# Two adaLN units of the first feed-forward summed on VectorE beside the first output product, with the conditioning row loaded earlier

## Chip, cores and metric

The kernel runs on one core of one Trainium2 chip. The metric is the device time of one execution in microseconds (us); the time before is 2353.25 us, the median of 3 runs (2352.32 to 2356.36).

## What is computed

One inference step of a two-layer backbone, for 128 prompt tokens (context pass) and 128 latent tokens (denoising) at once, D = 2048, all in fp32. Layer 0 mixes by MLA beside grouped-query attention with one input and one output projection, layer 1 by differential attention; each is followed by a gated convolutional feed-forward. Every sub-layer is modulated (adaLN) by shift, scale and gate, which are themselves a product of the conditioning vector:

```python
mod = jax.nn.silu(cond) @ w_ada[l] + b_ada[l]
sh1, sc1, gt1, sh2, sc2, gt2 = jnp.split(mod[:, None, :], 6, axis=-1)
h = rmsnorm(x, g_norm_mix[l]) * (1 + sc1) + sh1
m, new = mixer(h, ...)            # its last step is ... @ w_out_ab[i] in layer 0
x = x + gt1 * m
h = rmsnorm(x, g_norm_ffn[l]) * (1 + sc2) + sh2
x = x + gt2 * conv_ffn(h, w_ffn_up[l], w_ffn_conv[l], b_ffn_conv[l], w_ffn_down[l])
```

`cond` has two values, one for each group of tokens, so `mod` is two rows of 6 x 2048 numbers per layer.

## The kernel before, in words

**Products.** Activations lie feature-major: 16 blocks of 128 features by 256 tokens (128 prompt, 128 latent). Weights come as 1 MB tiles of 16 blocks 128x128 (`raw`, 3 buffers) by DMA from SyncE. Each fp32 value is kept as two float32r parts. For weights, `split` (L219) makes the high part on ScalarE (`wh`, the cast at L221) and the low part on VectorE (`wl`, a subtraction at L222), 8 blocks at a time, into 4 buffers of each; so half a product's weights are one cast and one split. `gemm` (L324) makes one output block of 128 features from 16 weight blocks with three matmuls each (L338 wh by high, L339 wh by low, L342 wl by high), 48 in all, into one of three accumulators `acc`. `residual` (L615) adds accumulator times gate to `x` on VectorE, two instructions at L617, which frees the accumulator; `stat_add` then squares and sums on ScalarE (L172) and GpSimd (L176).

**Modulation.** `mod` is cut into units (l, j, q): layer, which of the six vectors, which 512 of its 2048 numbers; j = 3 and 4 are shift and scale of the feed-forward, 5 its gate. A unit reads 4 tiles of 1 MB (`araw`, two buffers). There are two ways to make one.
- A *row unit* (list ROWS): TensorE multiplies the conditioning columns by each tile (`sum_rows`, L452: 4 matmuls a tile, which the profile shows as 8 records), then ScalarE copies the sum (L394), TensorE turns it by 4 transposes (L401), and VectorE reduces it (L403) and adds the bias (L411).
- A *feature unit* (list FEATS): VectorE multiplies each tile by the broadcast conditioning row and sums it over the free axis, one instruction per tile and row of `cond` (`feature_sum`, L429: 8 per unit, 128x2048 each, and a short read-out). It needs `condb`, the row on all partitions: `load_row` (L420) loads 2 MB (L422) and applies Silu on ScalarE in two instructions (L424). Early in the kernel the same memory serves as a tile buffer for row units (L498), last read by matmuls of L452.

**Pacing.** After each product `pump` (L515) advances row units by a rate of RATE and feature units by a rate of FRATE; RLIMIT and FLIMIT say how many units a stage may finish. `ensure` finishes what a stage needs. The order on each engine is then set by a scheduler, which places instructions by a simulated timeline; only what is marked to be kept in program order stays as written (among it load_row and feature_sum).

**The stages around the change.** In the in-projection (`mixer_ab`, quarter q == 3) the caches are loaded and the last quarter of the normed input is modulated. Then come the heads, then the first output product, out0 for short: 16 products in a loop, of which the last three are quiet (no pump) with the split in halves of a half (FINE). In these products the second half of the 16 blocks is consumed first (`first=8`), since the heads that make it are done first; products 0 to 2 begin beside the last heads. Then `modulated` hands over to the feed-forward: it finishes the statistics, makes one more row unit (0, 5, 0) in the gap (two tiles ahead of the new products), casts the modulated `hx` in 16 pieces, and runs three products at once (`first_three`), L324, L325 and L326. In the feed-forward, `up` calls load_row after its third block.

Of the kernel before, what the change touches and what calls it, by code (L numbers as in the profile page):

```python
# [10 lines left out]
F32 = mybir.dt.float32  # L11
F32R = mybir.dt.float32r
BF16 = mybir.dt.bfloat16
# [5 lines left out]
P = 128  # L19
D = 2048  # L20
KD = D // P
T = 128
NT = 2 * T
# [46 lines left out]
ROWS += [(0, j, q) for j in (2, 4, 3) for q in range(4)]  # L70
# [4 lines left out]
FEATS = [(0, 5, 1), (0, 5, 2), (0, 5, 3)]  # L75
# [3 lines left out]
RLIMIT = {"ab": 20, "ffn0": 21, "c": 32, "ffn1": 33}  # L79
FLIMIT = {"ab": 0, "ffn0": 12, "c": 12, "ffn1": 15}  # L80
SUMMED = [22, 23, 24, 26, 27, 28, 31]
# [4 lines left out]
def step_kernel(ctx: ExitStack, tc: tile.TileContext, A: dict):  # L86
# [346 lines left out]
    def feature_step():  # L433

        l, j, q = FEATS[feat["i"]]
        t, c = divmod(feat["t"], 2)
        if c == 0:
            feat["raw"] = T_(wpool, [P, 4, 512], "araw", bufs=2)
            sp.dma_start(out=feat["raw"], in_=A["w_ada"][l, j, q, t])
        feature_sum((l, j, q), t, c, feat["raw"],  # L440
                    T_(feat["pool"], [P, D], "junk").rearrange("p (g n) -> p g n", g=4))
# [243 lines left out]
    def mixer_ab(hx, rb0, st):  # L685
        l = 0
        with tc.tile_pool(name="ab", bufs=1) as ab:
            with tc.tile_pool(name="abp", bufs=1) as pj:
# [145 lines left out]
                for q in range(1, 4):  # L834
# [84 lines left out]
        ensure(l, 2)  # L919
        ada["pew"] = PEW["out0"]  # L920
        W = Weights(A["w_out_ab"], KD, 1)
        oh, ol = (lambda k: o[:, k, :NT]), (lambda k: o[:, k, NT:2 * NT])
        for c in range(KD):
            fine[0] = c >= KD - QUIET[1]
            residual(gemm(W.chunk(), oh, ol, first=8), l, 0, c, st)
            pump(RATE["out0"] if c < KD - QUIET[1] else 0)
# [124 lines left out]
    def ffn(hx, W, ready, todo, l, st):  # L1051
# [4 lines left out]
        with tc.tile_pool(name=f"ffn{l}", bufs=1) as fp, banks(f"pffn{l}") as pf:  # L1056
# [22 lines left out]
            def up(q):  # L1079
                gs = []  # L1080
                for i in range(q * KQ, (q + 1) * KQ):
# [11 lines left out]
                    if l == 0 and i == LATE - 1:  # L1093
                        load_row()
# [197 lines left out]
```

## Time and profile before

| | us |
|---|---|
| three runs, median (lowest to highest) | 2353.25 (2352.32 to 2356.36) |
| the profiled execution, its own time | 2353.05 |
| its span in the trace | 2351.3 |
| PE / weight loads / DVE / ACT / POOL busy | 2304.8 / 2190.2 / 1780.2 / 1163.3 / 144.8 |
| granted TensorE clock, mean | 0.993 |
| DMA, mean | 260 GB/s |

The span is what lies between the first and the last recorded instruction; the execution took 1.75 us more. PE is TensorE, PEld its weight loads, DVE VectorE, ACT ScalarE, POOL GpSimd, SP SyncE. In a timeline row stand the start, the time from start to end, the engine, line and operation, the tiles (`out<-in`), the shape and a count; behind it, if it waited, the idle time and what ended it. Matmuls overlap: one of 0.28 us starts every 0.11 us. So what an instruction costs TensorE is read from the distance of starts, not from its length.

### The profile page before, as it was taken

The numbers are of one execution on the slowest core, as the hardware profiler recorded it, in microseconds if no ns is written. First come the engines' busy times: TensorE is split into PE (matmuls) and PEld (weight loads), VectorE is DVE, ScalarE is ACT, GpSimd is POOL, SyncE is SP. The second block draws the span as 40 slices with busy tenths as digits, with TensorE's granted clock in tenths as the row PEclk, the third lists the DMA queues.
The fourth block names the chain that finished last, engine by engine and source line by source line (L and its number), as shares of the span: only waits on it lengthen the run. The fifth ranks groups of instructions, "written<-read, shape, count | busy, mean of one in ns | idle before, by whom it ended". The sixth has DMA issues, their size and how long they took to land. (4 is left out here: it accounts for less than half of the span.)

```text
span 2351.3 us, 47128 instructions
## 1 busy us (share of the span) xinstructions
PE 2304.8 (98%) x19654; PEld 2190.2 (93%) x19654; DVE 1780.2 (76%) x2662; ACT 1163.3 (49%) x1835; POOL 144.8 (6%) x133
## 2 busy tenths in 40 slices
PE   7999999999999999999999999999999999999997
PEld 6788878799999999999989999898999999999997
DVE  3667554579999999999968889887899755666654
ACT  4346553465554355554455555446555434555542
POOL 0002001100000000001220000022000000000011
PEclk9999999999999999999999999999999999999998
DMA  9887778777777877777767788786677555555553
GB/s 383 338 324 261 256 277 315 306 290 267 267 269 272 309 263 257 264 262 271 293 235 256 262 310 298 300 316 243 221 265 269 198 194 190 192 196 198 196 188 118
DMA packets 92421, 610.81 MB, mean 260 GB/s; under 512 B 9968, under 2 KB 17840, under 8 KB 20528
## 3 DMA queue, kind: packets, MB, share of 16 engines
q1 hardware_dynamic: 92208, 607.80, 70.2%
q8 instruction: 154, 2.52, 0.4%
q14 instruction: 59, 0.48, 0.1%
HBM read 603.01 MB, written 4.75 MB: 258 GB/s over the span
## 5 line engine op out<-in xcount | busy, mean ns | idle before, releaser
L221 ACT CAST wh<-raw 128x1024 fp32r<-128x1024 f32 (+1 forms) x788 | 793.4, 1013 | 947.5 <-PE acc L339 765.1
L222 DVE TENSOR_TENSOR wl<-raw,wh 128x1024 fp32r<-128x1024 f32 (+1 forms) x788 | 922.6, 1186 | 345.2 <-ACT wh L221 326.2
L338 PE MATMUL acc<-hx,wh 128*128 128x256 f32 x3808 | 1058.9, 279 | 5.6 <-ACT hx L568 4.6
L339 PE MATMUL acc<-hx,wh 128*128 128x256 f32 x3808 | 1056.4, 278 | 0.6 <-DVE hx L553 0.6
L342 PE MATMUL acc<-hx,wl 128*128 128x256 f32 x3808 | 1056.5, 278 | 0.0
L338 PEld LDWEIGHTS acc<-hx,wh 128*128 128x128 f32 x3808 | 715.8, 188 | 32.4 <-issue 10.9
L342 PEld LDWEIGHTS acc<-hx,wl 128*128 128x128 f32 x3808 | 716.1, 188 | 10.3 <-issue 9.2
L339 PEld LDWEIGHTS acc<-hx,wh 128*128 128x128 f32 x3808 | 716.8, 188 | 6.3 <-issue 5.0
L429 DVE CUSTOM_DVE_ANT_0 junk<-araw,condb 128x2048 f32<-128x2048 f32 (+1 forms) x176 | 404.0, 2295 | 0.0
L339 PE MATMUL acc<-g,wh 128*128 128x256 f32 x1408 | 388.3, 276 | 0.0
L342 PE MATMUL acc<-g,wl 128*128 128x256 f32 x1408 | 388.0, 276 | 0.0
L338 PE MATMUL acc<-g,wh 128*128 128x256 f32 x1408 | 387.8, 276 | 0.0
L339 PEld LDWEIGHTS acc<-g,wh 128*128 128x128 f32 x1408 | 264.3, 188 | 0.0
L342 PEld LDWEIGHTS acc<-g,wl 128*128 128x128 f32 x1408 | 264.1, 188 | 0.0
L338 PEld LDWEIGHTS acc<-g,wh 128*128 128x128 f32 x1408 | 264.0, 188 | 0.0
L176 POOL TENSOR_TENSOR sqacc<-sqacc,sq 128x256 f32<-128x256 f32 x62 | 83.4, 1344 | 1579.5 <-issue 1291.6
L1066 ACT ACTIVATE cv<-acc,convw 128x256 f32<-128x256 f32 x176 | 98.4, 559 | 3.6 <-PE acc L342 2.0
L617 DVE SCALAR_TENSOR_TENSOR x<-acc,mod,x 128x128 f32<-128x128 f32 x192 | 58.1, 344 | 54.7 <-PE acc L342 54.1
L1069 DVE SCALAR_TENSOR_TENSOR cv<-acc,convw,cv 128x254 f32<-128x254 f32 x176 | 83.8, 476 | 4.6 <-ACT cv L1066 4.6
L1072 DVE SCALAR_TENSOR_TENSOR cv<-acc,convw,cv 128x254 f32<-128x254 f32 x176 | 84.4, 480 | 3.7
L452 PE MATMUL ada<-araw,condw 128*32 128x512 f32 x576 | 79.3, 616 | 4.5 <-DMA araw<-w_ada 4.5
L303 PE MATMUL acc<-wh,hx 128*128 128x256 f32 x256 | 70.3, 281 | 0.9 <-ACT dv L977 0.9
(238 smaller groups left out, 2125.6 us busy)
## 6 DMA issues: line engine op xcount, KB each, us to landing
araw<-w_ada SPq DMA_DIRECT2D x178, 1024.0 KB, 5.5
raw<-w_up SPq DMA_DIRECT2D x176, 1024.0 KB, 4.8
raw<-w_down SPq DMA_DIRECT2D x88, 1024.0 KB, 4.8
raw<-w_in_c SPq DMA_DIRECT2D x48, 1024.0 KB, 6.0
raw<-w_in_ab SPq DMA_DIRECT2D x19, 1024.0 KB, 7.2
raw<-w_out_ab SPq DMA_DIRECT2D x16, 1024.0 KB, 6.9
raw<-w_out_c SPq DMA_DIRECT2D x16, 1024.0 KB, 6.1
condb<-w_ada SPq DMA_DIRECT2D x12, 1024.0 KB, 7.1
```

The source lines that it names most:

```text
L176: pool.tensor_tensor(out=st["acc"], in0=st["acc"], in1=sq, op=ALU.add)
L221: pin(act.copy(out_hi, src))
L222: pin(dve.tensor_tensor(out=out_lo, in0=src, in1=out_hi.bitcast(F32), op=ALU.subtract))
L303: pe.matmul(ps, hi, wh[:, s], start=a, stop=False)
L338: fixed(pe.matmul(ps[:, :n], wh, xh(k), start=(i == 0), stop=False))
L339: fixed(pe.matmul(ps[:, :n], wh, xl(k), start=False, stop=False))
L342: fixed(pe.matmul(ps[:, :n], wl, xh(k), start=False, stop=(i == last)))
L429: tc.keep_in_program_order(dve.tensor_tensor_reduce(out=junk, in0=raw, in1=condb[:, c].rearrange("p (g n) -> p g n", g=4), scale=1.0, scal ...
L452: i = pe.matmul(ada["ps"][32 * g:32 * g + 32, :], condw[:, 4 * t + g, :], raw[:, g], start=(t == 0), stop=(t == 3), skip_group_check=True)
L1066: pin(act.activation(y, ps, AF.Identity, scale=cw[:, 1, m:m + 1], bias=cw[:, 3, m:m + 1]))
L1069: pin(dve.scalar_tensor_tensor(out=y3[:, :, 1:], in0=p3[:, :, :T - 1], scalar=cw[:, 0, m:m + 1], in1=y3[:, :, 1:], op0=ALU.mult, op1=ALU.add))
L1072: pin(dve.scalar_tensor_tensor(out=y3[:, :, :T - 1], in0=p3[:, :, 1:], scalar=cw[:, 2, m:m + 1], in1=y3[:, :, :T - 1], op0=ALU.mult, op1=A ...
```

## The change

Units (0, 3, 2) and (0, 3, 3), half of the feed-forward's shift in layer 0, leave ROWS and become the first two of FEATS, so that they are summed by VectorE; their tiles in `w_ada` are laid out transposed by the host like those of other feature units. Limits and the indices in SUMMED shift by two. In out0 the row rate falls from 1.2 to 0.7 a product, and a feature rate of 1.3 comes in (16 sums over the 13 products that are not quiet). A pool `abo` around out0 holds two more `araw` buffers and the sums' unused output (`junk`, bf16). `ensure` for shift and scale of the feed-forward moves to the end of that loop. load_row moves from the third block of the feed-forward to the last quarter of the in-projection, right behind the loads of the caches. From there on, lines of the changed kernel are 1 to 3 higher.

```diff
-RATE = {"in": 0.5, "in3": 0.25, "heads": 0.85, "out0": 1.2, "c": 0.7, "outc": 0.7}
-FRATE = {"up": 0.7, "down": 1.42}
+RATE = {"in": 0.5, "in3": 0.25, "heads": 0.85, "out0": 0.7, "c": 0.7, "outc": 0.7}
+FRATE = {"out0": 1.3, "up": 0.7, "down": 1.42}
...
-ROWS += [(0, j, q) for j in (2, 4, 3) for q in range(4)]
+ROWS += [(0, j, q) for j in (2, 4) for q in range(4)] + [(0, 3, 0), (0, 3, 1)]
...
-FEATS = [(0, 5, 1), (0, 5, 2), (0, 5, 3)]
+FEATS = [(0, 3, 2), (0, 3, 3)]
+FEATS += [(0, 5, 1), (0, 5, 2), (0, 5, 3)]
...
-RLIMIT = {"ab": 20, "ffn0": 21, "c": 32, "ffn1": 33}
-FLIMIT = {"ab": 0, "ffn0": 12, "c": 12, "ffn1": 15}
+RLIMIT = {"ab": 18, "ffn0": 19, "c": 30, "ffn1": 31}
+FLIMIT = {"ab": 2, "ffn0": 14, "c": 14, "ffn1": 17}
...
-            feat["raw"] = T_(wpool, [P, 4, 512], "araw", bufs=2)
+            feat["raw"] = T_(feat["pool"] if l == 0 and j == 3 else wpool, [P, 4, 512], "araw", bufs=2)
...
                     if q == 3:
                         caches()
+                        load_row()
...
-        ensure(l, 2)
-        ada["pew"] = PEW["out0"]
-        W = Weights(A["w_out_ab"], KD, 1)
+        with tc.tile_pool(name="abo", bufs=1) as feat["pool"]:
+            ensure(l, 2)
+            ada["pew"] = PEW["out0"]
+            W = Weights(A["w_out_ab"], KD, 1)
...
-            residual(gemm(W.chunk(), oh, ol, first=8), l, 0, c, st)
-            pump(RATE["out0"] if c < KD - QUIET[1] else 0)
+                residual(gemm(W.chunk(), oh, ol, first=8), l, 0, c, st)
+                pump(*((RATE["out0"], FRATE["out0"]) if c < KD - QUIET[1] else (0,)))
+            ensure(l, 4)
+            ensure(l, 3)
...
-                    if l == 0 and i == LATE - 1:
-                        load_row()
```

How the order on the engines moves, at three places. First VectorE at the start of out0, before: residuals of the first products (`acc`) and splits of the next ones (`wl`).

```order
L617 SCALAR_TENSOR_TENSOR x_76<-acc_3848,mod_77,x_76 128x128 x2
L222 TENSOR_TENSOR wl_4064<-raw_4057,wh_4063 128x1024
L617 SCALAR_TENSOR_TENSOR x_76<-acc_3917,mod_77,x_76 128x128 x2
L222 TENSOR_TENSOR wl_4133<-raw_4130,wh_4132 128x1024
L617 SCALAR_TENSOR_TENSOR x_76<-acc_3987,mod_77,x_76 128x128 x2
L222 TENSOR_TENSOR wl_4137<-raw_4130,wh_4136 128x1024
L222 TENSOR_TENSOR wl_4207<-raw_4204,wh_4206 128x1024
L617 SCALAR_TENSOR_TENSOR x_76<-acc_4067,mod_77,x_76 128x128 x2
L222 TENSOR_TENSOR wl_4211<-raw_4204,wh_4210 128x1024
```

The same place after; `junk` is the unused output of a sum, and the second row of each pair is its read-out.

```order
L618 SCALAR_TENSOR_TENSOR x_76<-acc_3854,mod_77,x_76 128x128 x2
L430 ISA junk_3909,mod_77<-araw_3907,condb_82 128x2048
L430 ISA mod_77 128x1
L618 SCALAR_TENSOR_TENSOR x_76<-acc_3921,mod_77,x_76 128x128 x2
L223 TENSOR_TENSOR wl_4064<-raw_4057,wh_4063 128x1024
L618 SCALAR_TENSOR_TENSOR x_76<-acc_3993,mod_77,x_76 128x128 x2
L223 TENSOR_TENSOR wl_4132<-raw_4129,wh_4131 128x1024
L430 ISA junk_3981,mod_77<-araw_3907,condb_82 128x2048
L430 ISA mod_77 128x1
L223 TENSOR_TENSOR wl_4136<-raw_4129,wh_4135 128x1024
L223 TENSOR_TENSOR wl_4212<-raw_4209,wh_4211 128x1024
L430 ISA junk_4055,mod_77<-araw_4053,condb_82 128x2048
```

Sums now stand between the residuals and the splits; the first is directly behind the first residual, and the split `wl_4064`, which stood behind that residual, comes behind the sum and the second residual.

Second, TensorE at the hand-over, before: the tiles of a row unit (`araw`), the statistics (L201, L202), the spread of the scale over partitions (L216), and the feed-forward's first matmuls (L324).

```order
L452 MATMUL ada_5004<-araw_4784,condw_79 32x512 x4
L452 MATMUL ada_5004<-araw_5002,condw_79 32x512 x4
L201 MATMUL att_5039<-cst_74,sqacc_3899 128x1
L202 MATMUL att_5039<-cst_74,sq_5000 128x1
L216 MATMUL att_5056<-diag_5053,cst_74 128x256
L452 MATMUL ada_5004<-araw_5009,condw_79 32x512 x4
L452 MATMUL ada_5004<-araw_5015,condw_79 32x512 x4
L324 MATMUL acc_5168<-hx_5038,wh_5171 128x256
```

After, where L402 is the turn of unit (0, 3, 1) and `misc` the sum of unit (0, 5, 0):

```order
L453 MATMUL ada_4718<-araw_4791,condw_79 32x512 x4
L453 MATMUL ada_4718<-araw_5003,condw_79 32x512 x4
L202 MATMUL att_5028<-cst_74,sqacc_3905 128x1
L203 MATMUL att_5028<-cst_74,sq_5001 128x1
L402 MATMUL ada_5015<-cst_74,am_5013 128x128 x4
L217 MATMUL att_5045<-diag_5042,cst_74 128x256
L453 MATMUL misc_5037<-araw_5023,condw_79 32x512 x4
L325 MATMUL acc_5157<-hx_5027,wh_5160 128x256
L453 MATMUL misc_5037<-araw_5025,condw_79 32x512 x4
```

One tile of L453 is left between the spread and the first matmul L325, the next stands behind three of these, and the transposes of the unit before stand ahead of the spread.

Third, the loads that SyncE issues in the in-projection, before: `raw` are weights, `araw` modulation tiles, `vg` a cache.

```order
L704 DMA vg_236<-cache_gqa_v 128x256
L267 DMA raw_1789<-w_in_ab 128x2048
L267 DMA raw_1884<-w_in_ab 128x2048
L267 DMA raw_1983<-w_in_ab 128x2048
L469 DMA araw_1819<-w_ada 128x2048
L469 DMA araw_1915<-w_ada 128x2048
```

After:

```order
L705 DMA vg_236<-cache_gqa_v 128x256
L268 DMA raw_1792<-w_in_ab 128x2048
L268 DMA raw_1887<-w_in_ab 128x2048
L423 DMA condb_82<-condb 128x4096
L268 DMA raw_1986<-w_in_ab 128x2048
L470 DMA araw_1822<-w_ada 128x2048
L470 DMA araw_1918<-w_ada 128x2048
```

The 2 MB load of `condb` stands ahead of the weight load that was third. On ScalarE its two Silu instructions stand between the cast `wh_1893` of the tile before it and the statistics of the projection:

```order
L222 CAST wh_1889<-raw_1887 128x1024
L569 CAST hx_223<-nt_1780 128x256
L569 CAST hx_223<-nt_1786 128x256
L222 CAST wh_1893<-raw_1887 128x1024
L425 ACTIVATE condb_82<-condb_82 128x2048 x2
L170 ACTIVATE sqacc_1816<-proj_241 128x256
L720 ACTIVATE nt_1818<-proj_241,cst_74 128x256
L222 CAST wh_1988<-raw_1986 128x1024
```

More of the change, by code (lines that the diff above doesn't have):

```diff
@@ L437, in feature_step @@
         if c == 0:
-            feat["raw"] = T_(wpool, [P, 4, 512], "araw", bufs=2)
+            feat["raw"] = T_(feat["pool"] if l == 0 and j == 3 else wpool, [P, 4, 512], "araw", bufs=2)
             sp.dma_start(out=feat["raw"], in_=A["w_ada"][l, j, q, t])
         feature_sum((l, j, q), t, c, feat["raw"],
-                    T_(feat["pool"], [P, D], "junk").rearrange("p (g n) -> p g n", g=4))
+                    T_(feat["pool"], [P, 4, 512], "junk", BF16 if stage[0] == "ab" else F32))
         feat["t"] += 1
@@ L917, in mixer_ab @@
                 flush()
[L919 to L926 removed]
+        with tc.tile_pool(name="abo", bufs=1) as feat["pool"]:
+            ensure(l, 2)
+            ada["pew"] = PEW["out0"]
+            W = Weights(A["w_out_ab"], KD, 1)
+            oh, ol = (lambda k: o[:, k, :NT]), (lambda k: o[:, k, NT:2 * NT])
+            for c in range(KD):
+                fine[0] = c >= KD - QUIET[1]
+                residual(gemm(W.chunk(), oh, ol, first=8), l, 0, c, st)
+                pump(*((RATE["out0"], FRATE["out0"]) if c < KD - QUIET[1] else (0,)))
+            ensure(l, 4)
+            ensure(l, 3)
     def mixer_c(cp, hx, W, ready, todo, st):
```

2 lines of the change are left out of this document (1 added, 1 removed).

## Prediction, written before the changed kernel ran

> **What bounds the kernel now.** I read the page first (busy time of each engine, the chain that ended last), then the windows around the three places that the change touches, then single instructions there. The busy line:
>
> ```profile
> PE 2304.8 (98%) x19654; PEld 2190.2 (93%) x19654; DVE 1780.2 (76%) x2662; ACT 1163.3 (49%) x1835; POOL 144.8 (6%) x133
> PE 30%; issue 0%; DVE 0%; POOLq 0%; POOL 0%; ACT 0%; DVEq 0%; ACTq 0%
> ```
>
> TensorE (PE) is busy 98% of the span, VectorE (DVE) 76%. The chain that ended last, as far as it is followed back (30% of the span), is TensorE alone. What leaves TensorE is therefore time, if nothing that then feeds it is late. What may be late is read from the stages. The columns of the windows are busy us (x instructions) of PE, weight loads, DVE, ACT and POOL, then the granted clock, the DMA share and GB/s:
>
> ```profile
> 155.00:160.00 5.00, 5.00 (x44) 3.44 (x43) 3.03 (x6) 1.57 (x2) 0.00 (x0) 1.00 0.58 211
> 160.00:165.00 5.00, 5.00 (x40) 3.46 (x40) 1.96 (x4) 1.34 (x2) 0.00 (x0) 1.00 0.43 147
> 361.20:452.50 91.30, 91.30 (x765) 76.90 (x764) 44.39 (x73) 37.10 (x53) 17.77 (x14) 1.00 0.86 323
> 452.50:463.00 10.50, 7.55 (x45) 2.12 (x43) 7.91 (x22) 4.72 (x11) 2.30 (x3) 0.76 0.78 304
> 482.00:487.00 5.00, 5.00 (x47) 5.00 (x46) 4.08 (x6) 4.29 (x6) 0.00 (x0) 1.00 1.03 433
> 620.00:640.00 20.00, 20.00 (x179) 20.00 (x178) 18.87 (x25) 10.80 (x16) 0.00 (x0) 1.00 0.83 307
> ```
>
> From 361.2 (end of product 0) to 452.5 is the first output product: PE busy throughout at full clock, DVE 44.39 of 91.3, DMA at 0.86. From 452.5 to 463.0 is the hand-over to the feed-forward, where TensorE idles 3 us. At 620 to 640 TensorE issues 179 instructions in 20 us while DVE is busy 18.87 of 20 and sums features as it is to do here: a DVE at 94% has starved nothing there.
>
> **The row tiles that leave the output product.** What of those 91.3 us are modulation tiles:
>
> ```profile
> 361.20:452.50 91.30, 15.98 (x120) 2.36 (x120) 1.00 0.86 323
> 361.20:452.50 91.30, 2.39 (x16) 1.82 (x16) 1.00 0.86 323
> ```
>
> The first row holds L452 alone: 120 records, 8 to a tile, so 15 tiles. The second holds L401, the transposes: 16, so 4 units finish. What one costs TensorE, from the starts around it:
>
> ```profile
> 376.03 0.28 PE L342 MATMUL acc<-hx,wl 128*128 128x256 f32 x1
> 376.23 1.06 PE L452 MATMUL ada<-araw,condw 128*32 128x512 f32 x8
> 377.23 0.39 PE L338 MATMUL acc<-hx,wh 128*128 128x256 f32 x1
> 377.45 0.28 PE L339 MATMUL acc<-hx,wh 128*128 128x256 f32 x1
> ...
> 444.57 0.28 PE L338 MATMUL acc<-hx,wh 128*128 128x256 f32 x1
> 444.69 0.60 PE L401 MATMUL ada<-cst,am 128*128 128x128 f32 x4
> 445.04 0.37 PE L339 MATMUL acc<-hx,wh 128*128 128x256 f32 x1
> 445.25 0.28 PE L342 MATMUL acc<-hx,wl 128*128 128x256 f32 x1
> ```
>
> A product matmul takes a pitch of 20/178.5 = 0.112 us at 620 to 640; I use 0.1133. From 376.03 to 377.45 are 1.42 us, less two pitches 1.19 us per tile. From 444.57 to 445.25 are 0.68 us, less two pitches 0.45 us per four transposes. Check: the stretch has 765 - 120 - 16 = 629 product matmuls; 629 x 0.1133 + 15 x 1.19 + 4 x 0.45 = 90.9 of 91.3. So tiles are paid in full, and nothing else costs TensorE there. The order of the changed kernel holds 9 tiles and 2 turns in the same stretch: 6 x 1.19 + 2 x 0.45 = **8.0 us less**. The unchanged weight loads and matmuls stay.
>
> **The sums on VectorE.** Sixteen reductions come in: two units, four tiles, two rows. One costs:
>
> ```profile
> 361.33 0.61 DVE L617 SCALAR_TENSOR_TENSOR x<-acc,mod,x 128x128 f32<-128x128 f32 x2 [0.82 <-PE acc L342]
> 362.29 1.22 DVE L222 TENSOR_TENSOR wl<-raw,wh 128x1024 fp32r<-128x1024 f32 x1 [0.35 <-ACT wh L221]
> 363.43 0.60 DVE L617 SCALAR_TENSOR_TENSOR x<-acc,mod,x 128x128 f32<-128x128 f32 x2
> 363.95 1.22 DVE L222 TENSOR_TENSOR wl<-raw,wh 128x1024 fp32r<-128x1024 f32 x1
> 365.08 0.60 DVE L617 SCALAR_TENSOR_TENSOR x<-acc,mod,x 128x128 f32<-128x128 f32 x2
> ...
> 368.02 1.30 DVE L222 TENSOR_TENSOR wl<-raw,wh 128x1024 fp32r<-128x1024 f32 x1 [1.20 <-ACT wh L221]
> ...
> 565.60 2.29 DVE L429 CUSTOM_DVE_ANT_0 junk<-araw,condb 128x2048 f32<-128x2048 f32 x1
> 567.80 0.14 DVE L429 DVE_READ_ACCUMULATOR2_ANT mod<- 128x1 f32 x1
> ```
>
> A sum with its read-out takes 2.2 us from start to the next instruction (565.60 to 567.80), a split 1.14 (362.29 to 363.43), a residual 0.52 (363.43 to 363.95). Sixteen sums are 35.2 us; two fewer reductions give back some 1. Products 0 to 2, whose first halves ran beside the heads, end together near 361 to 365; the sums fall beside products 3 to 13, which last 11 x 48 x 0.1133 + 9 x 1.19 + 2 x 0.45 = 71.4 us, some 75 with the first 4. Beside them stand DVE's 44.39 less two products' share (629/48 = 13.1 products, 3.4 us each), 37.6, plus 34: 72 of 75, 96%. That fits, barely, so order counts. A split must come after the cast that the freed buffer lets start, and before the product that reads it.
>
> The first sum stands right behind the first residual, ahead of residuals 1 and 2 and of the split that product 3 reads first. Residual 1 frees the accumulator that product 4 takes. In the rows above that split starts at 362.29 and a split follows each residual with no more than 0.35 us of slack, so 2.2 us more and one residual put it near 365, when the first products have about run out. I take **+1.5**; nothing is the lower end (no split was due), and the upper is a sum and a split, 2.2 + 1.14 = 3.4.
>
> Walking the later order with these durations, each split comes 0.1 to 3 us ahead of its product, least at products 4 (0.1), 15 (0.6) and 5 (1.2). Two margins lie near the 0.35 and 1.20 us that a split waits for its cast above, so I take another **+1.5**, from 0 to 5 (four products late by a cast's 1.2 each).
>
> The sums' tiles have two buffers of their own, free once the heads' tiles are:
>
> ```profile
> 350.64 0.16 DVE L646 SCALAR_TENSOR_TENSOR nmx<-mx,rsmla 128x2 f32<-128x2 f32 x1
> ...
> araw<-w_ada SPq DMA_DIRECT2D x20, 1024.0 KB, 6.1
> ```
>
> The last head's maximum is done near 350.8 and its exponentials follow, so I put the first load's issue near 352; 6.1 us (median from 340 to 460) is 358, before its use at 361.9. Later ones have, by the same walk, 11 to 14 us from issue to use. I cost the loads at nothing; the bytes are those that the row tiles had.
>
> **The hand-over.** Before, two tiles stand ahead of the feed-forward's first matmul, each waiting for its transfer:
>
> ```profile
> 458.61 1.94 PE L452 MATMUL ada<-araw,condw 128*32 128x512 f32 x8 [0.85 <-DMA araw<-w_ada]
> 461.10 1.93 PE L452 MATMUL ada<-araw,condw 128*32 128x512 f32 x8 [0.56 <-DMA araw<-w_ada]
> 462.96 1.01 PE L324 MATMUL acc<-hx,wh 128*128 128x256 f32 x3
> 463.77 0.41 PE L325 MATMUL acc<-hx,wh 128*128 128x256 f32 x1
> ...
> 459.81 1.31 ACT L568 CAST hx<-nt 128x256 fp32r<-128x256 f32 x4
> ...
> 476.31 1.70 POOL L553 TENSOR_TENSOR hx<-nt,hx 128x256 fp32r<-128x256 f32 x1 [2.79 <-ACT hx L568]
> ...
> 480.59 0.28 PE L325 MATMUL acc<-hx,wh 128*128 128x256 f32 x1
> ```
>
> The first hx piece is cast by some 460.2, so the first product waits 2.8 us for tiles, not for data. In the changed order one tile stands there, and 3 matmuls run ahead of the next. By its rows that is a tile of 1.93 less; with the turn that now sits in the gap, the start moves 0.9 earlier. The two further tiles and the turn that followed inside the first products leave: 2 x 1.19 + 0.45 = 2.8. Together 3.7 at most. The floor is the modulation itself: the last low part of hx ends at 478.0 and is read at 480.59, so about 2.6 can be taken up before TensorE waits for it. I take **-2.7**, from 0 (the modulation is later by as much) to -3.7.
>
> [...]
>
> **The conditioning row in the in-projection.** One 2 MB load and two activations move from the feed-forward's up-products:
>
> ```profile
> L424 ACT ACTIVATE condb<-condb x2: 1905/1908/1912, 506.4 to 508.3; 128x2048 f32<-128x2048 f32 x2
> ...
> L452 PE MATMUL ada<-condb,condw x96: 592/592/686, 55.9 to 156.8; 128*32 128x512 f32 x96
> ...
> 174.03 1.05 ACT L221 CAST wh<-raw 128x1024 fp32r<-128x1024 f32 x1
> 177.39 1.05 ACT L221 CAST wh<-raw 128x1024 fp32r<-128x1024 f32 x1 [2.30 <-PE acc L339]
> ...
> DMA to landing us min/median/max: 13.7/13.7/13.7
> ```
>
> The last matmul that reads the tile's old contents starts at 156.8, so the load starts near 157 to 158 and falls in stretches with DMA at 0.58 and 0.43; at its old place it took 13.7 us to land. On SyncE it stands ahead of one weight load, which waits with it for at most the 1 us. The activations, 2 x 1.91 = 3.8 us, stand behind the cast of 174.03 and ahead of that of 177.39, where ACT idles 2.30. The next casts are then 2 to 4 us late; of the four buffers, each 24 x 0.1133 = 2.7 us of matmuls, two stand ready and leave TensorE a lead of some 5.4. I take **+0.5**, between 0 (the lead covers all) and 3.8 (nothing does). What the feed-forward gains I put at 0: TensorE runs at pace there (47 matmuls in 5 us with that very load in flight), and its sums start no earlier.
>
> **Sum.** -8.0 + 1.5 + 1.5 - 2.7 + 0.5 = -7.2 us. The profiled execution took 2353.05 us, the median of the three runs is 2353.25: 2353.05 - 7.2 = **2345.9 us**. All costs at their low ends: -11.7, 2341.3; all at their high ends: -8.0 + 3.4 + 5 + 0 + 3.8 = +4.2, 2357.3.
>
> **Rivals.** A: the gain is half given back. DVE at 96% runs a few splits behind their sums and the products wait for DVE instead of tiles: three or four products late by 1.2 to 1.5 us, 5 us back beside the terms above, 2351. For it speaks the thin margin; against it the stretch at 620, at 94% without loss. B: slower. A sum waits at the head of DVE's queue for its tile, and every split and residual waits behind it, which no row tile on TensorE could do to them. It decides once a load takes longer than the 11 us that it has: at the 13.7 us of the conditioning row, 2.7 x 8 tiles = 21 us, 2353 - 7.2 + 21 = 2367. Against it stands the median of 6.1; for it, that the same bytes in 6.5 us less raise the DMA share from 0.86 to 0.93. The row at 482 shows 433 GB/s for 5 us, so there is room above the 323 of the stretch, which is why B stays at 0.12. [...] C: the move does nothing, because tiles fill time in which TensorE waited anyway: 2353. The check of 90.9 in 91.3 speaks against it.
>
> **Chances.** Forecast 0.60 (2341 to 2348), A 0.22, B 0.12, C 0.03, better than every low end 0.03. The range leaves out B and the edges: 2341.0 to 2354.0. A measurement of this kernel tells some 0.2%, 4.7 us, from no change. Faster by more: the forecast, the better case and a little of A, 0.66; within it: most of A, and C, 0.22; slower: B, 0.12.
>
> **What would show it.** Right: the stretch from the first residual to the last product is about 85 to 88 us, with 72 L453 records instead of 120 and DVE busy 93% or more; L453 ahead of the first feed-forward matmul costs one tile. The early stall shows as one or two us idle of PE released by wl near 365. Wrong: more PE idle released by wl after 370 (A), DVE idle released by araw transfers (B), or casts in the in-projection that PE waits for near 180.

## The result, and the profile after

The changed kernel takes 2345.51 us (median of 7 executions, 2344.03 to 2350.39); the kernel before, run beside it, 2353.68 us (median of 7). The ratio is 0.9968, 95% interval [0.9959, 0.9977]: 7.5 us less, between 5.4 and 9.6. The profiled execution of the changed kernel has a span of 2343.7 us against 2351.3. The busy line of its page:

```profile
PE 2295.5 (98%) x19582; PEld 2189.7 (93%) x19582; DVE 1817.6 (78%) x2692; ACT 1162.2 (50%) x1833; POOL 144.9 (6%) x133
```

TensorE has lost 9.3 us of work (2304.8 before), VectorE has gained 37.4 (1780.2 before). To see where the time went, I cut the kernel at three starts that both traces have: the first and the last residual of the output product (L617 before, L618 after), and the fourth convolution of the feed-forward (L1066, L1071). Between the first two lies the output product, between the last two the hand-over. The last two rows of before:

```profile
452.76 0.60 DVE L617 SCALAR_TENSOR_TENSOR x<-acc,mod,x 128x128 f32<-128x128 f32 x2
...
492.02 0.56 ACT L1066 ACTIVATE cv<-acc,convw 128x256 f32<-128x256 f32 x1
```

The same cuts after, with the first residual:

```profile
359.84 0.61 DVE L618 SCALAR_TENSOR_TENSOR x<-acc,mod,x 128x128 f32<-128x128 f32 x2 [0.82 <-PE acc L343]
...
444.66 0.61 DVE L618 SCALAR_TENSOR_TENSOR x<-acc,mod,x 128x128 f32<-128x128 f32 x2 [2.12 <-PE acc L343]
...
483.56 0.56 ACT L1071 ACTIVATE cv<-acc,convw 128x256 f32<-128x256 f32 x1
```

| stretch | before | after | change |
|---|---|---|---|
| start to the first residual | 361.33 | 359.84 | -1.5 |
| output product | 91.43 | 84.82 | **-6.6** |
| hand-over, to the fourth convolution | 39.26 | 38.90 | -0.4 |
| from there to the end of the span | 1859.2 | 1860.2 | +0.9 |

The first row is spread between executions: kernels of this study that differ only behind that point reach their first residual between 359.84 and 362.65. So is the last one (1857.6 to 1865.2 over all runs). The output product repeats: it took 91.43 and 91.42 in two kernels without the sums, 84.82 to 84.84 in three with the order of the changed one and 85.22 in a fourth. The hand-over took 39.26 and 39.63 in the two kernels without the sums, so a change of 0.4 there can't be told from none. The windows of the changed kernel over the output product, over its middle, and over the 8 us in which the feed-forward's first matmuls start:

```profile
359.80:444.70 84.90, 83.57 (x713) 74.54 (x715) 80.73 (x102) 34.14 (x49) 17.70 (x14) 1.00 0.90 356
370.00:440.00 70.00, 70.00 (x600) 63.24 (x600) 69.31 (x87) 27.77 (x41) 14.66 (x11) 1.00 0.92 365
450.00:458.00 8.00, 6.20 (x28) 2.54 (x28) 7.93 (x22) 5.37 (x15) 2.16 (x3) 0.57 0.79 309
```

In the middle VectorE is busy 69.31 of 70 us and TensorE 70 of 70: a VectorE at 99% holds nothing up here. The only idle time of TensorE in the output product is 1.33 us at its start (84.90 - 83.57):

```profile
363.03 1.06 PE L453 MATMUL ada<-araw,condw 128*32 128x512 f32 x8 [1.33 <-DMA araw<-w_ada]
```

It waits there for a row tile's transfer, not for a split. SyncE's rows tell why: the first two tiles of the sums were issued right ahead of that tile's load.

```profile
350.42 0.80 SPq L440 DMA_DIRECT2D araw<-w_ada  x2
353.71 0.33 SPq L470 DMA_DIRECT2D araw<-w_ada  x1
```

The load of 353.71 landed 9.3 us later, near 363.0; at the same place before, it took 4.8 (issued at 355.30, 6.5 us behind the load before it).

The hand-over of the changed kernel on TensorE, rows that wait and the tiles:

```profile
449.39 0.70 PE L217 MATMUL att<-diag,cst 128*128 128x256 f32 x2 [1.43 <-DVE diag L209]
450.61 1.85 PE L453 MATMUL misc<-araw,condw 128*32 128x512 f32 x8 [0.52 <-DMA araw<-w_ada]
453.73 1.01 PE L325 MATMUL acc<-hx,wh 128*128 128x256 f32 x3 [1.27 <-ACT hx L569]
454.67 1.94 PE L453 MATMUL misc<-araw,condw 128*32 128x512 f32 x8
456.54 0.58 PE L326 MATMUL acc<-hx,wh 128*128 128x256 f32 x1
...
465.33 1.06 PE L453 MATMUL misc<-araw,condw 128*32 128x512 f32 x8
466.33 0.39 PE L325 MATMUL acc<-hx,wh 128*128 128x256 f32 x1
...
474.79 0.28 PE L327 MATMUL acc<-hx,wl 128*128 128x256 f32 x1
475.79 0.36 PE L339 MATMUL acc<-hx,wh 128*128 128x256 f32 x1 [0.72 <-DVE cv L1077]
```

The same stretch before, from the first matmul of the three products to the fourth product, with the tiles and the turn in it:

```profile
462.96 1.01 PE L324 MATMUL acc<-hx,wh 128*128 128x256 f32 x3
...
467.12 0.60 PE L401 MATMUL ada<-cst,am 128*128 128x128 f32 x4
...
471.06 1.07 PE L452 MATMUL misc<-araw,condw 128*32 128x512 f32 x8
...
474.31 1.07 PE L452 MATMUL misc<-araw,condw 128*32 128x512 f32 x8
...
478.80 1.07 PE L452 MATMUL misc<-araw,condw 128*32 128x512 f32 x8
...
484.33 0.28 PE L338 MATMUL acc<-hx,wh 128*128 128x256 f32 x1
```

The first matmul of the feed-forward starts 9.07 us behind the last residual, where it was 10.20 (462.96 - 452.76): 1.1 us earlier. The fourth product starts only 0.4 us earlier (31.13 us behind the last residual, 31.57 before), although one tile and one turn fewer stand between. Three things take this up. From the tile at 454.67, at a granted clock of 0.50 (450.8 to 457.6), to the next matmul are 1.87 us, where the tile at 465.33, at 1.00 (464 to 467), takes 1.00. The matmuls of the three products start every 0.1178 us, most of them before every 0.1133. And the fourth product waits 0.72 us for an accumulator: it starts 1.00 us behind the last matmul of the three, 0.11 before.

### The profile page after: what moved, and what is told of

Same layout as the page of the kernel before. It is cut to its first block, busy times and chain, and to the rows that moved or that the text cites. A ratio compares the mean times of both kernels' runs of the same rounds, so it can differ in the third digit from the quotient of the medians.

```text
span 2343.7 us, 47002 instructions
## 1 busy us (share of the span) xinstructions
PE 2295.5 (98%) x19582; PEld 2189.7 (93%) x19582; DVE 1817.6 (78%) x2692; ACT 1162.2 (50%) x1833; POOL 144.9 (6%) x133
## 5 line engine op out<-in xcount | busy, mean ns | idle before, releaser
L430 DVE CUSTOM_DVE_ANT_0 junk<-araw,condb 128x2048 f32<-128x2048 f32 (+1 forms) x192 | 442.9, 2307 | 0.1
L1071 ACT ACTIVATE cv<-acc,convw 128x256 f32<-128x256 f32 x176 | 98.2, 558 | 1.4 <-PE acc L327 1.4
L618 DVE SCALAR_TENSOR_TENSOR x<-acc,mod,x 128x128 f32<-128x128 f32 x192 | 58.0, 343 | 42.5 <-PE acc L343 41.7
L453 PE MATMUL ada<-araw,condw 128*32 128x512 f32 x512 | 68.6, 603 | 4.2 <-DMA araw<-w_ada 4.2
```

The lines of the kernel that those rows point to most:

```text
L430: tc.keep_in_program_order(dve.tensor_tensor_reduce(out=junk, in0=raw, in1=condb[:, c].rearrange("p (g n) -> p g n", g=4), scale=1.0, scal ...
L453: i = pe.matmul(ada["ps"][32 * g:32 * g + 32, :], condw[:, 4 * t + g, :], raw[:, g], start=(t == 0), stop=(t == 3), skip_group_check=True)
L1071: pin(act.activation(y, ps, AF.Identity, scale=cw[:, 1, m:m + 1], bias=cw[:, 3, m:m + 1]))
```

## The experiments

The theory: the gain is the row tiles that left TensorE in the output product, and the sums lie wholly beside matmuls. The rivals: sums that hold up splits unseen; a gain or a loss of the moved conditioning row; a gain from the hand-over. Eleven kernels were run, each beside the kernel before.

| kernel | median us | ratio to before, interval | output product | hand-over |
|---|---|---|---|---|
| before | 2353.68 | | 91.43 | 39.26 |
| changed | 2345.51 | 0.9968 [0.9959, 0.9977] | 84.82 | 38.90 |
| row_early_only | 2354.71 | 1.0003 [0.9994, 1.0012] | 91.42 | 39.63 |
| short_sums | 2346.27 | 0.9964 [0.9952, 0.9975] | 84.20 | 39.10 |
| one_load | 2348.13 | 0.9977 [0.9969, 0.9986] | 85.44 | 41.61 |
| late_start | 2345.01 | 0.9966 [0.9954, 0.9979] | 83.74 | 40.35 |
| one_unit | (see there) | 1.0039 [1.0004, 1.0074] | 89.32 | 39.17 |
| sums_half_more | 2356.10 | 1.0005 [0.9996, 1.0013] | 90.53 | 43.04 |
| one_buffer | 2356.18 | 1.0009 [1.0001, 1.0018] | 85.12 | 48.79 |
| warm | 2347.30 | 0.9970 [0.9961, 0.9979] | 85.22 | 41.92 |
| turn10 | 2347.12 | 0.9965 [0.9952, 0.9977] | 84.84 | 37.18 |
| warm_strict10 | 2346.00 | 0.9962 [0.9949, 0.9976] | 84.83 | 39.87 |
| warm_strict10_late | 2348.16 | 0.9972 [0.9962, 0.9982] | 83.78 | 42.70 |

The two stretches are from the starts in one trace of each kernel, as above. Unless it is said otherwise, an edit is against the changed kernel.

### The conditioning row alone

`row_early_only`, an edit of the kernel before:

```diff
                     if q == 3:
                         caches()
+                        load_row()
...
-                    if l == 0 and i == LATE - 1:
-                        load_row()
```

> The kernel before with only the conditioning row's load and its two activations moved to the in-projection; no unit changes sides. In the changed kernel the first residual of the output product starts at 359.84 us, 1.49 us earlier than before (361.33), although the prediction gave this move a cost of 0.5. Theory: the move is worth nothing by itself, since the casts behind the activations come 1.5 to 2.6 us late but TensorE shows no idle time there; the 1.49 us come from the order of the row tiles (552 records ahead of that residual instead of 556) and from a tile that was waited for at 322. Then the ratio lies in 0.9990 to 1.0010 and the first residual at 361.0 to 361.8. Rival 1: the move itself saves the 1.5 us: first residual at 359.6 to 360.2, and the ratio is near 0.9994. Rival 2: it costs 0.5 to 3.8 us as bounded in the prediction, and the change pays it elsewhere.

The ratio is 1.0003 [0.9994, 1.0012]. The output product is as before, the hand-over 0.4 us longer, and TensorE waits for nothing from 155 to 215 us. The first residual came at 362.08, 0.75 us later than before; with the changed kernel's 359.84 on the other side, both are spread, and the theory's account of the 1.49 us by the order of tiles isn't borne out either. From the fourth convolution to the 41st, the stretch of the feed-forward that the load and the activations left, are 201.74 us in both. So the move by itself costs and gains nothing that shows, to within the interval, some 2 us.

### Sums cut to a sixteenth

`short_sums`:

```diff
+        n = 32 if l == 0 and j == 3 else 512
         tc.keep_in_program_order(dve.tensor_tensor_reduce(
-            out=junk, in0=raw, in1=condb[:, c].rearrange("p (g n) -> p g n", g=4), scale=1.0, scalar=0.0,
+            out=junk[:, :, :n], in0=raw[:, :, :n],
+            in1=condb[:, c].rearrange("p (g n) -> p g n", g=4)[:, :, :n], scale=1.0, scalar=0.0,
```

> The changed kernel, but the sixteen sums of the two units read 128 of the 2048 elements of a tile's row only, so most of the sum is left out; the loads stay. It takes some 14 x 2.2 = 31 us of work from VectorE in the output product and nothing else. Theory: the sums lie wholly beside the matmuls, so the time is that of the changed kernel within 1 us (about 2345, ratio 0.996 to 0.9975 to before), and TensorE's wait of 1.33 us near 363, which the trace puts down to the transfer of a row tile, is still there. Rival: sums at 96% of VectorE make splits late in a way that the records hide: 2 to 4 us faster than the changed kernel, 2341 to 2343.

```profile
360.35:444.60 84.25, 83.38 (x712) 74.34 (x714) 47.44 (x102) 33.73 (x50) 16.26 (x14) 1.00 0.89 358
```

VectorE falls from 80.73 to 47.44 us and the output product from 84.82 to 84.20. Thirty-three us of work on VectorE cost 0.6 us. The rival of hidden losses falls. But the wait at 363 didn't stay as expected: it is 0.87 us, and now a split ends it.

```profile
363.08 0.38 PE L343 MATMUL acc<-hx,wl 128*128 128x256 f32 x1 [0.87 <-DVE wl L223]
```

### One load for all sums, and sums that begin later

`one_load`:

```diff
-            feat["raw"] = T_(feat["pool"] if l == 0 and j == 3 else wpool, [P, 4, 512], "araw", bufs=2)
-            sp.dma_start(out=feat["raw"], in_=A["w_ada"][l, j, q, t])
+            if l or j != 3 or (q, t) == (2, 0):
+                feat["raw"] = T_(feat["pool"] if l == 0 and j == 3 else wpool, [P, 4, 512], "araw", bufs=2)
+                sp.dma_start(out=feat["raw"], in_=A["w_ada"][l, j, q, t])
```

> The changed kernel, but only the first of the eight tiles of the two units is loaded, and all sixteen sums read it, so seven tiles' sums are of the wrong data; 7 MB of transfers are left out. Theory: TensorE's wait near 363 (1.33 us in the changed kernel) comes from the two tile loads that stand ahead of a row tile's on SyncE (issued 350.4 and 350.8, the row tile's 353.7 and landed 9.3 us later); with one of them gone the row tile lands some 2.5 us earlier and the wait is gone: 1.3 us less, about 2344. Rival: the first sum, behind the first residual, makes the wait, as the prediction had it: it stays at 1 to 1.5 us. The other six loads were costed at nothing: no more than 0.5 us beyond the 1.3.

`late_start`:

```diff
-FRATE = {"out0": 1.3, "up": 0.7, "down": 1.42}
+FRATE = {"out0": 1.46, "up": 0.7, "down": 1.42}
...
-                pump(*((RATE["out0"], FRATE["out0"]) if c < KD - QUIET[1] else (0,)))
+                pump(*((RATE["out0"], FRATE["out0"] if c > 1 else 0) if c < KD - QUIET[1] else (0,)))
```

> The changed kernel with the sums paced only from the third product on (1.46 a product instead of 1.3), so that no sum stands ahead of the residuals of products 1 and 2 and of the split that product 3 reads first. The two loads still stand ahead of the row tile's on SyncE. Theory: the wait of TensorE near 363 is the row tile's transfer, so it stays, 1 to 1.5 us, and the time is that of the changed kernel within 1 us. Rival (the prediction's term of +1.5): the wait goes with the early sum, 1.5 us less. The denser sums behind leave less slack: if the margins of 0.1 to 1.2 us were real, TensorE shows new waits for wl, 1 to 4 us in sum.

With all but one of the sums' loads gone, the row tile is no longer waited for. But TensorE stands still nearly as long, now behind the first sum, for the accumulator that residual 1 frees and for the split:

```profile
363.63 0.35 PE L339 MATMUL acc<-hx,wh 128*128 128x256 f32 x1 [0.44 <-DVE x L619]
363.82 0.28 PE L340 MATMUL acc<-hx,wh 128*128 128x256 f32 x1
364.67 0.38 PE L343 MATMUL acc<-hx,wl 128*128 128x256 f32 x1 [0.57 <-DVE wl L223]
```

That is 1.0 us; with two more late splits behind (0.39), TensorE idles 1.40 us in the output product. The time is not the 2344 that was expected but 2348.13, mostly by the hand-over, 41.61 us, where TensorE waits 3.05 us for an accumulator. With the later start, 0.45 us is left, and the output product is 1.1 us shorter (83.74). So two waits lie over one another: take the transfer away and the sum's queue shows, worth 1.0 us; take the early sum away, and the order has the tile's matmuls at 365.17, when it has landed. What the transfer would cost alone, no run shows. The theory that the transfer alone makes the wait falls, and so does its rival; the expectation that the wait stays in late_start failed. The rest of the gain of late_start is lost in the hand-over, where its last sum ends 1.7 us, not 9.4, before the last residual, and TensorE waits 2.98 us for hx. No new waits for splits came of the denser sums.

### One unit in place of two

`one_unit` (rates, limits and indices change with it):

```diff
-ROWS += [(0, j, q) for j in (2, 4) for q in range(4)] + [(0, 3, 0), (0, 3, 1)]
+ROWS += [(0, j, q) for j in (2, 4) for q in range(4)] + [(0, 3, 0), (0, 3, 1), (0, 3, 2)]
...
-FEATS = [(0, 3, 2), (0, 3, 3)]
+FEATS = [(0, 3, 3)]
```

> Only unit (0, 3, 3) is summed on VectorE, (0, 3, 2) stays a row unit on TensorE (rates 0.95 and 0.65). Theory: the gain is the row tiles' time on TensorE, so half of it comes: 3 to 4 tiles of 1.19 us and one turn of 0.45 leave the output product, about -4 us against before: 2349 to 2350, ratio 0.9980 to 0.9987, and VectorE is busy some 75% of the product instead of 95%. Rival: VectorE at its limit takes part of the second unit's gain, or the gain is mostly in the hand-over: then one unit gives as much as two, 2345 to 2347.

Six of its twelve executions took 2346.5 to 2350.7 us and six 2374 to 2380; the interval mixes both and says nothing, and why half of them are 27 us longer stays open. The profile is of one of 2347.28. There the output product is 89.32 us: 12 tiles stand in it instead of 15, and 3 turns instead of 4, so 3 x 1.19 + 0.45 = 4.0 us less, and TensorE waits 2.02 us for a tile at 363. 91.43 - 4.0 + 2.0 = 89.4. VectorE is busy 72% of it. The sum of tiles less the early wait holds at one unit as at two, and half a change pays the whole early wait. The time does not follow as well: the median of the six shorter executions is 2347.8, below the 2349 to 2350 that were expected and within 1 us of the rival's range, while the two stretches are only 2.2 us shorter than before; the rest lies outside them and stays open.

### Half as many sums again

`sums_half_more` (the lines of the call are only indented):

```diff
-        tc.keep_in_program_order(dve.tensor_tensor_reduce(
...
+        for _ in range(2 if l == 0 and j == 3 and c == 0 else 1):
+            tc.keep_in_program_order(dve.tensor_tensor_reduce(
...
```

> The changed kernel with each sum of the first row of cond done twice (the same result): 8 more sums, 8 x 2.2 = 17.6 us more on VectorE beside the same matmuls. VectorE is busy 69.3 of 70 us from 370 to 440 in the changed kernel, yet TensorE shows no idle there. Theory: two units are all that fits; VectorE becomes the bound, and the output product grows by 10 to 17 us less what the three quiet products take up: the time is 2352 to 2361, and TensorE waits for wl and x. Rival: there is slack that the busy share doesn't show (the last three products, starts held back by the residuals), and the loss is under 4 us, 2345 to 2349.

```profile
360.60:451.20 90.60, 87.08 (x730) 75.86 (x728) 90.60 (x110) 37.75 (x53) 22.22 (x14) 1.00 0.91 343
```

VectorE is busy in all of the stretch. The 17.6 us more cost 5.7 us in the output product and 4.1 in the hand-over, whose modulation stands behind four sums that weren't done: 9.8 us in all, against 10 to 17 less what the quiet products take up. Two units fill VectorE, 69.31 of 70 us in the changed kernel. Eight more sums are what a third unit would bring: by these numbers they would cost more than the four tiles and the turn that it would take from TensorE (4 x 1.19 + 0.45 = 5.2 us), an estimate; no such kernel was run.

### One buffer for the sums' tiles

`one_buffer`:

```diff
-            feat["raw"] = T_(feat["pool"] if l == 0 and j == 3 else wpool, [P, 4, 512], "araw", bufs=2)
+            feat["raw"] = T_(feat["pool"] if l == 0 and j == 3 else wpool, [P, 4, 512], "araw", bufs=1 if l == 0 and j == 3 else 2)
```

> The changed kernel with one buffer for the sums' tiles instead of two: a load can be issued only after the second sum of the tile before it, and takes 7 to 11 us here. This prices rival B of the prediction, a sum that waits for its tile at the head of VectorE's queue. A tile's turn is 13 / 8 products, some 10 us, of which the two sums leave 3 to 5 for the load. Theory: seven loads are late by 2 to 6 us each; what VectorE, busy 99%, loses there TensorE loses nearly one for one: 10 to 30 us slower than the changed kernel, 2355 to 2375. Rival: splits that are placed between take up the wait, under 4 us, 2345 to 2349.

It is 10.7 us slower than the changed kernel (9.6 by the ratios), at the low end of what was expected, but not by the way that was expected. Of the sixteen sums only two waited for their tile, 0.55 and 1.41 us, and the output product is 0.3 us longer. The order held the sums back instead, and four of them were left for the hand-over, two of them ahead of its scale and its modulation:

```profile
448.20 2.28 DVE L430 CUSTOM_DVE_ANT_0 junk<-araw,condb 128x2048 bf16<-128x2048 f32 x1
450.42 0.08 DVE L430 DVE_READ_ACCUMULATOR2_ANT mod<- 128x1 f32 x1
450.42 0.15 DVE L185 TENSOR_SCALAR rv<-att 128x2 f32<-128x2 f32 x1
450.49 0.18 DVE L404 TENSOR_REDUCE mod<-ada 128x8 f32<-128x32 f32 x1
450.59 2.28 DVE L430 CUSTOM_DVE_ANT_0 junk<-araw,condb 128x2048 bf16<-128x2048 f32 x1
```

The other two, behind a load issued at 452.94, came at 465.0 and 468.8, and with them the shift that the last modulated pieces need. The hand-over is 9.9 us longer. So the late sums were paid where the next stage needs their result.

### The hand-over: clock, accumulator, order

Three edits to the changed kernel, alone and together. `warm`:

```diff
+        fill = att_bank()
+        if not fixed:
+            for _ in range(4):
+                pe.matmul(fill[:, :256], ident, st["last"], start=True, stop=True)
-        rb = spread(diagonal(r, (0, 1)), bank=att_bank)
+        dg = diagonal(r, (0, 1))
+        rb = spread(dg, bank=att_bank)
+        if not fixed:
+            for _ in range(4):
+                pe.matmul(fill[:, :256], ident, dg, start=True, stop=True)
```

> The changed kernel with 8 matmuls of 128x256 that compute nothing of use in the gap of the hand-over (4 behind the statistics, 4 behind the spread). In the changed kernel the granted clock is half from about 450.8 to 457.6, 3.9 us of which lie behind the feed-forward's first matmul at 453.7 (1.9 us before the change), so this was to cost the hand-over 1 us of the 2.7 that were predicted. Theory: with TensorE kept busy the clock stays at full in the gap, the first products run at 0.113 instead of 0.21 us a matmul and a tile costs 1.06 instead of 1.94, and the third of the first products ends 1.5 to 2.5 us earlier after the last residual than in the changed kernel. Whether the next product gains too is open: if its accumulator (VectorE's conv steps) is the bound, the fourth conv stays at 38.9 us behind the last residual, and the time is that of the changed kernel within 1 us; if not, it is up to 2 us less. Rival: the clock falls all the same, and nothing moves.

```profile
450.00:458.00 8.00, 6.32 (x42) 3.87 (x41) 7.50 (x20) 3.64 (x10) 1.70 (x2) 1.00 0.79 310
478.00:484.00 6.00, 5.92 (x35) 4.98 (x36) 3.72 (x8) 3.52 (x7) 0.00 (x0) 0.72 0.82 318
```

The clock does as the theory says: 1.00 from 450 to 458, where it was 0.57. From the first to the last matmul of the three products are 19.33 us, in the changed kernel 21.06 (453.73 to 474.79): 1.7 us less. They start 0.8 us later (9.90 us behind the last residual, 9.07 there), so the last of them ends 0.9 us earlier, less than the 1.5 to 2.5 that were expected; the third convolution on ScalarE comes 31.88 us behind the last residual, 32.16 in the changed kernel. But then TensorE stops for the fourth product's accumulator, and the clock falls there instead (0.72 from 478 to 484):

```profile
455.47 0.62 PE L325 MATMUL acc<-hx,wh 128*128 128x256 f32 x3 [1.68 <-ACT hx L569]
...
474.80 0.28 PE L327 MATMUL acc<-hx,wl 128*128 128x256 f32 x1
478.08 0.36 PE L339 MATMUL acc<-hx,wh 128*128 128x256 f32 x1 [3.00 <-ACT cv L1079]
```

The hand-over is 3.0 us longer than without fillers. In this kernel's order the first of the three products ends 11 matmuls ahead of the third, in the changed kernel 24, and two steps of the convolution on VectorE, with a split between them, must read the accumulator before it is free (the second ends at 477.94; the row names a step of ScalarE that ends at 478.02). The lead alone does not decide: it is 24 matmuls before the change too, without a wait, and 24 in `row_early_only`, which has no sums in this stage and waits 2.16 us at this place. So such a wait comes with the order that the scheduler finds, not with the sums alone. What sets the lower clock off is not shown. In the changed kernel it is 0.50 for 6.8 us, from 450.8 to 457.6, and TensorE's longest idle times ahead of that are 1.43 and 0.52 us; with the fillers 1.68 us of idle time stand in the stretch at 1.00, and 3.00 us ahead of the one at 0.72.

`turn10`, the second edit alone:

```diff
-IN_TURN = ([(c, k) for k in range(12) for c in range(3)] + [(c, k) for c in range(3) for k in range(12, KD)])
+IN_TURN = ([(c, k) for k in range(10) for c in range(3)] + [(c, k) for c in range(3) for k in range(10, KD)])
```

> The changed kernel with the three first products of the feed-forward sharing the first 10 of 16 blocks in turn instead of the first 12, so that the first of them ends some 40 matmuls (4.5 us) ahead of the third instead of 24 (2.7 us). The fourth product needs the accumulator of the first, which two steps of the convolution on VectorE and one on ScalarE must have read. In the changed kernel TensorE waits 0.72 us there, and 3.0 us where the order of the kernel with fillers left 11 matmuls between. Theory: the hand-over's gain was lost at this accumulator; with the longer lead the wait is gone and the fourth conv starts 38.0 to 38.4 us behind the last residual (38.9 in the changed kernel, 39.3 before): 0.5 to 0.9 us less in all. Rival: the modulation holds the first product back by as much (waits for hx appear), and nothing is gained.

The wait is gone, and VectorE frees the first accumulator before the fourth product asks for it:

```profile
472.10 0.47 DVE L1074 SCALAR_TENSOR_TENSOR cv<-acc,convw,cv 128x254 f32<-128x254 f32 x1
472.60 0.48 DVE L1077 SCALAR_TENSOR_TENSOR cv<-acc,convw,cv 128x254 f32<-128x254 f32 x1
```

The fourth convolution comes 37.18 us behind the last residual, 1.7 us earlier than in the changed kernel and more than was expected, though TensorE now waits 2.16 us for the first hx instead of 1.27. The accumulator is 0.9 of it: the fourth product starts 0.11 us behind the last matmul of the three, not 1.00. The other 0.8 lies in the three products themselves, 20.30 us instead of 21.06: the matmuls start every 0.1133 us instead of 0.1178, and the granted clock from 450 to 458 is 0.83 instead of 0.57. Nothing shows that the edit brings this. In the total the gain can't be told: 2347.12 us (2343.81 to 2348.93).

The third edit writes the order out. `warm_strict10` has it with both others, and `warm_strict10_late` has that of `late_start` besides:

```diff
-                         AS_MADE if fixed else IN_TURN, lambda: sum_rows(2, raws[2]), fixed)
+                         AS_MADE if fixed else IN_TURN, lambda: sum_rows(2, raws[2]), True)
```

> As before, with the eight filler matmuls in the gap and the order of the three first products written out (first 10 blocks in turn), so that the first one ends 36 matmuls (4.1 us) ahead of the third. With the fillers alone the clock stayed at full, but TensorE then waited 3.0 us for the fourth product's accumulator and the clock fell there, and the time was that of the changed kernel. Theory: clock and accumulator are the two things that took the hand-over's predicted 2.7 us; with both out of the way the fourth conv starts 36.5 to 37.5 us behind the last residual instead of 38.9, and the time is 1.5 to 2.5 us below the changed kernel's, some 2343 to 2344, ratio 0.9955 to 0.9962. Rival: the modulation is the floor: TensorE waits for hx instead, and the fourth conv stays at 38.5 or later.

> The kernel of the run before, with the sums paced from the third product on (1.46 a product), which took 0.9 us of wait off the start of the output product when it was tried alone. Theory: the two add: 0.5 to 1 us less than the run before, 2342 to 2343.5. Rival: the denser sums run into the hand-over (VectorE comes later to the modulation, as it did alone: 2.98 us of waits for hx), and it is no better or worse than the run before.

Neither does what was expected. The written order with fillers has no wait for the accumulator, but waits for splits of the first products' second halves (1.47 us), the granted clock is 0.50 from 470.0 to 473.4, and the products start 0.8 us later, as with the fillers alone: 39.87. With the later sums on top it is 42.70, by 3.02 us of waits for casts, 1.28 for splits and 1.52 for a tile. Each cover that was taken away in the hand-over showed the next thing behind it. No kernel here is shown to beat the changed one; turn10 has the shortest hand-over.

## Why the prediction was right, point by point

The time was forecast at 2345.9 and is 2345.5. The mechanism that carries the sum, tiles paid in full beside a VectorE that keeps up, is what the runs show. That the total came so near is luck: the hand-over gave 2.3 us less than forecast, and three costs that did not come in full, 1.5, 0.5 and 0.2, gave nearly that back.

- **Tiles, -8.0: right.** The trace of the changed kernel has 9 tiles and 2 turns between the first and the last residual, where 15 and 4 were. 8.0 less the idle 1.33 is 6.7; measured 6.6. One unit gave 4.0 less 2.0, measured 2.1.
- **Early stall, +1.5: right in size, half right in cause.** 1.33 us, within 0 to 3.4. The prediction named the split behind the first sum. The trace shows a row tile behind the sums' own loads, which had been costed at nothing since "the bytes are those that the row tiles had": their number is the same, their moment is not. With one of those loads gone the sum's queue cost 1.0 us.
- **Thin margins, +1.5: mis-sized, 0.** From 370 to 440 TensorE has no idle time with VectorE at 99%, and cutting the sums to a sixteenth gained 0.6 us in the output product, less than the early stall. The margins of 0.1 to 1.2 us held.
- **Hand-over, -2.7: mis-sized, -0.4.** The start came 1.1 us earlier (0.9 forecast); the 2.8 us that were to leave the first products did not come. First, the count: two units are 8 tiles, and 6 had been taken off in the output product and one ahead of the first matmul, so one could leave here and not two. The traces show it, three tiles before and two after, so a tile and a turn, 1.6 us. Then what stood against it: a tile at half the clock (1.87 us instead of 1.00), the wider pitch (143 x 0.0045 = 0.6) and the accumulator (1.00 us instead of 0.11), 2.4 us together. 1.1 + 1.6 - 2.4 = 0.3, measured 0.4. The floor of the term was read from the last low part of hx alone; the accumulator was not looked for. The half-rate clock is not in the sum: in `warm`, with the clock at 1.00 from 450 to 458 instead of 0.57, the three products took 1.7 us less (19.33 instead of 21.06), and a start 0.8 us later and a wait of 3.00 us for the accumulator took it away again.
- **Conditioning row, +0.5: nothing** (ratio 1.0003 [0.9994, 1.0012]), within its bounds; the runs tell it to some 2 us.
- **Rivals.** A (half given back on VectorE): refuted by the shortened sums. B (a sum at the head of VectorE's queue waiting for its tile): not met, as the sums' loads took 6.8 to 11.2 us and none was waited for by VectorE, at 365 GB/s from 370 to 440; with one buffer its price appeared at the hand-over, 9.9 us, rather than as 2.7 us a tile. C (tiles that fill time in which TensorE waits anyway): wrong in the output product; in the hand-over it isn't tested, as no run put a tile back there.

The two stretches give -6.6 - 0.4 = -7.0 us; the spread of the rest adds -0.6 in this pair of traces (-1.5 ahead of them, +0.9 behind).

## What to carry to other kernels

The work that left TensorE was paid back in full only where nothing else was due in the same moment: of 8.0 us of tiles and turns 6.6 came in the output product, where 1.33 went to a wait, and of 2.7 us (1.1 and 1.6) 0.4 in the hand-over. So price such work by the distance of starts inside a stretch without idle time, count it in one stretch only, and at a stage's edge ask what it was covering. VectorE ran at 99% (69.31 of 70 us) beside a TensorE without idle time, with its work there ahead of time; where four sums were left over for the next stage, the hand-over was 9.9 us longer (`one_buffer`) or 4.1 (`sums_half_more`). Loads that are moved count by their moment too: behind two others a load took 9.3 us here, 4.8 without them.

## What was not expected of the hardware

A sum on VectorE took 2.28 or 2.82 us. In the changed kernel's output product five of the sixteen take 2.82; each of those started while a GpSimd addition still had 0.67 us to run, and none of the others did (one met the last 0.05 us). Where the addition started during a sum, it was the addition that took longer, 2.45 and 2.55 us; the others took 0.74 to 1.18. GpSimd's addition from 365.42 to 366.58, and the sums without and with one:

```profile
365.42 1.16 POOL L177 TENSOR_TENSOR sqacc<-sqacc,sq 128x256 f32<-128x256 f32 x1 [0.52 <-ACT sq L173]
```

```profile
360.37 2.28 DVE L430 CUSTOM_DVE_ANT_0 junk<-araw,condb 128x2048 bf16<-128x2048 f32 x1
...
365.91 2.82 DVE L430 CUSTOM_DVE_ANT_0 junk<-araw,condb 128x2048 bf16<-128x2048 f32 x1
```

In `short_sums` even the sums of 128 elements range from 0.28 to 0.83 us, by the same 0.55. Why a sum and an addition take longer side by side isn't shown; the five sums took 0.54 us more each.

In these two traces matmuls start at two pitches at a granted clock of 1.00: every 0.1133 us, and every 0.1178 in stretches such as 458 to 474 of the changed kernel and 364 to 372 of before. Over the 144 matmuls of the first three products that is 0.6 us. What sets it isn't shown.
